# Masks on VectorE, a softmax in three visits and values spread over one stage, in a hybrid decoder step

## The chip, the cores and the metric

One core of one Trainium2 chip runs the kernel. The metric is the device time of one launch in microseconds; the median of the runs counts. Five engines work side by side and meet at semaphores: PE (TensorE, matmuls), DVE (VectorE), ACT (ScalarE), POOL (GpSimd) and SP (SyncE, which only issues DMAs here). Each engine works through its own instructions in a fixed order.

## The reference

One layer of a decoder in which stick-breaking attention and a gated short convolution run in parallel, for one prompt of 512 tokens (with 16 learned tokens ahead) and for 8 sequences that each decode 4 tokens over 512 past positions, which lie in pages of 128. All is float32.

```python
h = rmsnorm(x, g_pre)
q, k, v, ga, cb, cc, ch, gc, ma, mc = jnp.split(h @ w_in, split_offsets(), axis=-1)   # w_in: 2048 x 12288
a = attend(q, k, v, b_sb).reshape(bsz, t, D_ATTN) * jax.nn.silu(ga)
u = cc * ch
u_ext = jnp.concatenate([conv_hist.astype(u.dtype), u], axis=1)
c = cb * causal_conv(u_ext, w_conv, b_conv) * jax.nn.silu(gc)
merged = (jax.nn.sigmoid(ma + b_gate[:D_MODEL]) * (a @ w_pa)
          + jax.nn.sigmoid(mc + b_gate[D_MODEL:]) * (c @ w_pc))
y = x + rmsnorm(merged @ w_out, g_post)
...
def stick_breaking(q, k, v, q_pos, k_pos, b_sb):
    z = jnp.einsum('bqhd,bkhd->bhqk', q, k) * HEAD_DIM ** -0.5 + b_sb[None, :, None, None]
    mask = k_pos[None, :] < q_pos[:, None]
    log_keep = jnp.where(mask, jax.nn.log_sigmoid(-z), 0.0)
    after = lax.cumsum(log_keep, axis=3, reverse=True) - log_keep
    attn = jnp.where(mask, jnp.exp(jax.nn.log_sigmoid(z) + after), 0.0)
    return jnp.einsum('bhqk,bkhd->bqhd', attn, v)
```

D_MODEL is 2048, there are 8 heads of 128, w_pa and w_pc are 1024 x 2048 and w_out is 2048 x 2048. The keys and values of the decoded sequences come from a paged cache through page_table.

## The kernel before, in words

The tokens lie along the free axis: 512 prompt rows and 32 decode rows, 544 queries (TQ). Every float32 operand is split into a high part, rounded to the format that TensorE takes at full rate, and a low part. A product of weights and tokens is then three matmuls: high by high, high by low, low by high. Each weight tile of 128 x 1024 is loaded by SP (w_load), rounded by a ScalarE copy into whi (L235), and VectorE subtracts it to get wlo (L236). TensorE needs both. This split goes on through the whole kernel: 377 such tiles.

The stages, in order:

- Start: norm of the rows, transposes, the first q products. The change does not touch it.
- Heads 0 to 3 are projected and attended at once (head_now); of heads 4 to 7 the projections are stored to DRAM (head_later). In the same time the first of the decode's logits are computed.
- Gates and convolution: the columns of w_in for ga, cb, cc, ch, gc, ma and mc, two column tiles at a time (pair), by a scheme of seven half-size products in place of eight (seven, with the matmuls in product, L849). The sigmoids of ma and mc (ScalarE, L994) go to the DRAM tensor gate_scr.
- The w_pc stage: 16 column tiles (j), each of 48 products in two halves of 272 tokens (L251), which VectorE multiplies with the gate tile gt (L1063) that SP loaded, and which GpSimd's queue writes back to gate_scr (L1064). At j = 0, 3, 6 and 9 the attention of heads 4, 5, 6 and 7 is worked in (HERE, head_here).
- The w_pa stage: the same with the attention's result a_hl; GpSimd's queue loads the two gates' tile back (L1081), which waits for the write of L1064 to the same place.
- The w_out stage (seven again, L849), the transposes back to rows (rows), the squares, and in finish the last norm, the addition of x and the output's DMAs.

The decode part is a Python generator, decode_steps, whose pieces are called in between, so that its instructions land between the products of other stages:

- Logits (L638 to L671): for each sequence and page, q by k as elementwise products on VectorE (L658) and sums on ScalarE and VectorE.
- Softmax in the stick-breaking sense (L672 to L722). For the new rows z_new (32 x 256) and the four pages z_all (128 x 1024) softplus_parts runs on ScalarE: Abs (L404), Exp (L405), Ln (L406), Relu (L407), with the sums on VectorE. Then follow triangular matmuls and an Exp. ScalarE holds one set of function tables at a time: an ACT_TABLE_LOAD stands ahead of a function whose set is not loaded. The Sigmoids of the gates lie in another set than Exp and Ln.
- Values (L724 to L762): 32 pages of values in four blocks (two groups of four sequences, two halves of the heads). Each page is loaded by GpSimd's queue into one of eight vpage buffers. For each of the four sequences of a group a page's matmul (L747) writes its own 32 of the 128 rows of one PSUM tile.

How often the generator is called sets where these pieces stand. During the gates dec_group is called 36 times; the first 29 calls drive one or two pieces of the logits each, the 30th everything up to and with the softmax. In the w_pc stage dec_step(2) runs in each of the 16 steps of j.

The attention of one head (attend, L522): the z products for three groups of key blocks B, C and A, then for each group the softplus steps, the causal mask, and the split into hi (L423) and lo; sums over the later blocks; the products with neg_u and neg_one (L593), which subtract the log sums behind each key; then Exp, the mask again, the split, and the o products with v (L603). The mask is a GpSimd instruction (L550) that sets what is not earlier than the query to zero. Ten masks a head are needed: five blocks, each in r and in A. GpSimd's instructions and the DMAs that it issues stand in one queue.

The planner that orders instructions within an engine keeps a given order where the code pins it (keep_in_program_order, pin).

## Time and profile before

| | |
|---|---|
| median of 3 runs | 1661.16 us (1659.37 to 1664.0) |
| the profiled execution | 1663.13 us, its span 1661.5 us |
| mean granted clock of TensorE | 0.981 |
| busy share of the span | PE 96%, DVE 75%, ACT 59%, POOL 16% |
| moved by DMA | 252.72 MB, mean 152 GB/s |

The span is what the trace covers; the execution's own time is 1.6 us longer. The profile's page gives the busy time of each engine, the span in 40 slices of 41.5 us, the chain of work that ended last, and the costliest groups of instructions. In rows of the trace stand the time in us, the busy time, the engine, the line, the operation, output<-input and the number of instructions; in square brackets the idle time before and what ended it.

### The profile page before, as it was taken

To read this page: it belongs to the slowest core of one execution; us is meant where nothing else is said; L and a number is where in the kernel's file an instruction comes from. 1 tells how busy PE (TensorE), PEld (TensorE's weight loads), DVE (VectorE), ACT (ScalarE), POOL (GpSimd) and SP (SyncE) were. 2 spreads that over 40 slices of the span, in tenths; PEclk is the share of its full clock that TensorE was granted. 3 is DMA by queue.
4 is the path that set the end of the run, shared out by engine and by line. 5 is a ranking of instruction groups with operands and counts; after the bars stand their busy time and mean duration, and the time that the engine had idled before them with its cause. 6 is when DMAs were issued, how large, how long until landed. Compare 5 with 4: busy or idle time off the path is not lost. (4 is left out here: it accounts for less than half of the span.)

```text
span 1661.5 us, 31640 instructions
## 1 busy us (share of the span) xinstructions
PE 1600.6 (96%) x12174; PEld 1540.7 (93%) x12174; DVE 1252.6 (75%) x1669; ACT 974.8 (59%) x2532; POOL 262.7 (16%) x460
## 2 busy tenths in 40 slices
PE   7999999999999999999999999899999979999995
PEld 6999999999999999999999999888878969999995
DVE  4538888797979898988878888865466647877775
ACT  6247887746765656565667677953445533445552
POOL 0033233222101010000011011031232210000002
PEclk7999999999999999999999999999999989999998
DMA  9255545435544444444455454355895535433335
GB/s 225 77 177 155 155 144 160 143 119 171 174 131 128 128 134 129 129 133 134 135 157 170 148 166 143 103 185 163 283 317 169 170 99 174 154 111 94 94 105 193
DMA packets 307468, 252.72 MB, mean 152 GB/s; under 512 B 11569, under 2 KB 276853, under 8 KB 306213
## 3 DMA queue, kind: packets, MB, share of 16 engines
q1 hardware_dynamic: 279269, 161.90, 34.0%
q0 software_dynamic: 28016, 88.80, 16.3%
q8 instruction: 95, 1.56, 0.4%
q14 instruction: 56, 0.46, 0.1%
q10 hardware_dynamic: 32, 0.01, 0.0%
HBM read 217.95 MB, written 32.71 MB: 151 GB/s over the span
## 5 line engine op out<-in xcount | busy, mean ns | idle before, releaser
L235 ACT CAST whi<-raw 128x1024 fp32r<-128x1024 f32 x251 | 262.8, 1049 | 259.7 <-PE o L849 74.3
L236 DVE TENSOR_TENSOR wlo<-raw,whi 128x1024 fp32r<-128x1024 f32 x251 | 306.1, 1220 | 75.6 <-ACT whi L235 57.4
L849 PE MATMUL mm<-h_hi,whi 128*128 128x272 f32 (+1 forms) x1152 | 333.9, 290 | 6.2 <-ACT whi L235 6.2
L849 PE MATMUL mm<-h_lo,whi 128*128 128x272 f32 (+1 forms) x1152 | 332.4, 289 | 0.0
L849 PE MATMUL mm<-h_hi,wlo 128*128 128x272 f32 (+1 forms) x1152 | 332.0, 290 | 0.0
L849 PE MATMUL o<-t_hi,whi 128*128 128x272 f32 (+1 forms) x864 | 253.7, 294 | 7.4 <-DVE c L875 3.0
L849 PE MATMUL o<-t_hi,wlo 128*128 128x272 f32 (+1 forms) x864 | 251.2, 291 | 1.3 <-DVE wlo L236 1.3
L849 PE MATMUL o<-t_lo,whi 128*128 128x272 f32 (+1 forms) x864 | 251.2, 291 | 0.0
L236 DVE TENSOR_TENSOR wlo<-s,whi 128x1024 fp32r<-128x1024 f32 x126 | 154.0, 1222 | 101.3 <-ACT whi L235 101.0
L849 PEld LDWEIGHTS mm<-h_hi,whi 128*128 128x128 f32 x1152 | 217.4, 189 | 10.8 <-ACT whi L235 7.8
L849 PEld LDWEIGHTS mm<-h_lo,whi 128*128 128x128 f32 x1152 | 216.8, 188 | 2.5 <-issue 2.5
L849 PEld LDWEIGHTS mm<-h_hi,wlo 128*128 128x128 f32 x1152 | 216.4, 189 | 2.8 <-issue 2.5
L664 ACT ACTIVATE junk<-pr 128x128 f32<-128x128 f32 x592 | 182.7, 309 | 29.2 <-DVE pr L658 13.4
L235 ACT CAST whi<-s 128x1024 fp32r<-128x1024 f32 x126 | 131.6, 1045 | 100.1 <-PE o L849 32.2
L251 PE MATMUL mm<-h_hi,whi 128*128 128x280 f32 (+1 forms) x640 | 187.1, 293 | 0.0
L251 PE MATMUL mm<-h_hi,wlo 128*128 128x280 f32 (+1 forms) x640 | 187.1, 293 | 0.0
L251 PE MATMUL mm<-h_lo,whi 128*128 128x280 f32 (+1 forms) x640 | 186.7, 292 | 0.0
L849 PEld LDWEIGHTS o<-t_hi,whi 128*128 128x128 f32 x864 | 164.2, 190 | 16.5 <-issue 5.0
L849 PEld LDWEIGHTS o<-t_hi,wlo 128*128 128x128 f32 x864 | 164.4, 190 | 2.3 <-DVE wlo L236 2.2
L849 PEld LDWEIGHTS o<-t_lo,whi 128*128 128x128 f32 x864 | 164.9, 191 | 0.0
L658 DVE TENSOR_TENSOR pr<-kpage,qb 128x1024 f32<-128x1024 f32 x128 | 152.2, 1217 | 7.7 <-DMA kpage<-in_cache_k 3.4
L251 PEld LDWEIGHTS mm<-h_hi,whi 128*128 128x128 f32 x640 | 120.5, 188 | 0.7
(384 smaller groups left out, 3436.2 us busy)
## 6 DMA issues: line engine op xcount, KB each, us to landing
raw<-in_w_in SPq DMA_DIRECT2D x192, 512.0 KB, 4.2
kpage<-in_cache_k POOLq DMA_DIRECT2D x64, 256.0 KB, 3.4
qb<-q_scr POOLq DMA_DIRECT2D x32, 512.0 KB, 5.5
vpage<-in_cache_v POOLq DMA_DIRECT2D x64, 256.0 KB, 5.7
raw<-in_w_out SPq DMA_DIRECT2D x32, 512.0 KB, 4.0
gate_scr<-g POOLq DMA_DIRECT2D x32, 272.0 KB, 3.4
gt<-gate_scr POOLq DMA_DIRECT2D x16, 544.0 KB, 4.1
raw<-in_w_pc SPq DMA_DIRECT2D x16, 512.0 KB, 7.2
```

Source lines behind the costliest of these rows:

```text
L235: act.copy(hi, x)
L236: dve.tensor_sub(lo, x, hi.bitcast(F32))
L251: pe.matmul(o, lhsT=w, rhs=r[:, t0:t1], start=(k == 0 and n == 0), stop=(k == nk - 1 and n == 2))
L658: dve.tensor_mul(pr, kt.unsqueeze(1).broadcast_to([P, 2, 512]), qt))
L664: act.activation(junk, pr[:, t, h * P:(h + 1) * P], AF.Copy, accum_out=z_all[:, pg, b, 4 * hf + h, 2 * i + t:2 * i + t + 1])
L849: pe.matmul(o, lhsT=l[:, k, :], rhs=r, start=(start and k == 0 and m == 0), stop=(stop and k == 7 and m == 2), skip_group_check=True)
```

## The change

It has these parts.

- **Masks on VectorE.** For heads 4 to 7 the mask is one scalar_tensor_tensor on VectorE: the minimum with 3e38, times a tile of zeros and ones (after, which is neg_u plus one). Heads 0 to 3 keep the GpSimd masks.
- **Softplus at one go.** For heads 4 to 7 the four ScalarE steps of all three groups come first, pinned in that order (twelve instructions); the sums, masks and splits follow. softplus_parts is cut in two for that (softplus_acts, softplus_sums). The output's PSUM tile is zeroed by ScalarE, not VectorE.
- **Early inputs.** Head 4's k, q and v are loaded from SP's queue inside the gate stage (at j + w = 14), not behind it; their pool opens when the logits are done, on the side of memory where the decode's tiles lie.
- **The logits at an even rate.** dec_group drives them for 31 calls at the same rates as before; the 32nd call runs what is left of them and the first visit of the softmax.
- **Softmax in three visits**, one for each further call of dec_group: the new rows with pages 3 and 2; pages 1 and 0; the Exps on z_new and on the whole of z_all. Each visit begins with a preload of the tables for Exp and Ln, and its ScalarE steps are pinned.
- **Values spread over w_pc.** dec_step(1 + j % 2) runs in each step, not dec_step(2): 24 calls in 16 steps where 32 were offered. The vpage buffers are seven, not eight.
- **The end.** The 32 rows left over (REST) are transposed into a PSUM tile of their own and kept as 4 strips of 32 rows by 512 columns, so that their addition is one instruction of 128 x 512; their scale is spread over the strips by one small matmul. All additions of finish run on VectorE, in cuts of 1024 or 512 columns; ScalarE and GpSimd share none. The output's DMAs alternate between the queues of SP and ScalarE.

```diff
@@ attend
-                if w > 0:
+                if w > 0 and after is not None:
+                    xm = x[:m, c0:c0 + w]
+                    dve.scalar_tensor_tensor(out=xm, in0=xm, scalar=BIG, in1=after[:m, ts - st * P:ts - st * P + w],
+                                             op0=ALU.min, op1=ALU.mult)
+                elif w > 0:
...
         for g in GROUPS:
-            zt = gt[g]
-            e, l, r, t = tl("e", g), tl("l", g), tl("r", g), tl("lo", g)
-            softplus_parts(e, l, r, t, zt, b)
+            elr[g] = tl("e", g), tl("l", g), tl("r", g)
+            if after is not None:
+                softplus_acts(*elr[g], gt[g], b, pin)
+        for g in GROUPS:
+            (e, l, r), t = elr[g], tl("lo", g)
+            if after is None:
+                softplus_acts(e, l, r, gt[g], b)
+            softplus_sums(e, l, r, t)
             mask(r, g)
...
-        dve.memset(ot, 0.0)
+        if after is None:
+            dve.memset(ot, 0.0)
+        else:
+            act.copy(ot, zero_c.broadcast_to([P, PQ]))
@@ decode_steps
-            tc.keep_in_program_order(act.preload_act_table_set(LNEXP))
...
-            softplus_parts(e[:TS, :BHT], l[:TS, :BHT], rn, t[:TS, :BHT], zn, zero_c[:TS])
-            softplus_parts(e, l, r, t, zf, zero_c)
...
+            for p0 in (2, 0):
+                pin(act.preload_act_table_set(LNEXP))
+                if p0:
+                    softplus_parts(e[:TS, :BHT], l[:TS, :BHT], rn, t[:TS, :BHT], zn, zero_c[:TS], pin)
+                    mask_new(rn)
+                c = slice(p0 * BHT, (p0 + 2) * BHT)
+                softplus_parts(e[:, c], l[:, c], r[:, c], t[:, c], zf[:, c], zero_c, pin)
...
+                yield
+            pin(act.preload_act_table_set(LNEXP))
+            pin(act.activation(zn, zn, AF.Exp))
             mask_new(zn)
-            yield
...
+            pin(act.activation(zf, zf, AF.Exp))
...
-                            vt = d3.tile([P, 512], F32, name="vpage", bufs=8)
+                            vt = d3.tile([P, 512], F32, name="vpage", bufs=7)
@@ dec_group
-        if n <= 29:
+        if n <= 31:
             dec_step(1 if 4 < n <= 20 else 1 + n % 2, "logits")
-        elif n == 30:
-            dec_step(64, "weights")
+        elif n == 32:
+            dec_step(64, "logits")
+            dec_step(1)
@@ gates, w_pc
+            if j + w == 14:
+
+                after = hl[0].tile([P, P], F32, name="after")
+                dve.tensor_scalar_add(after, neg_u.bitcast(F32), 1.0)
+                loaded = head_loads(NOW)
...
-        dec_step(2)
+        dec_step(1 + j % 2)
@@ rows, finish
-                square(4, j, pt[:REST, n:n + P], REST)
-                dve.tensor_mul(og_rest(cs), pt[:REST, n:n + P], g[:REST])
+                square(4, j, pr, REST)
+                r0, c0 = j // 4 * REST, j % 4 * P
+                dve.tensor_mul(ogr[r0:r0 + REST, c0:c0 + P], pr, g[:REST])
...
+                for c0, c1 in zip(cuts[b], cuts[b][1:]):
+                    xc = xs_[i][:, c0:c1]
+                    dve.scalar_tensor_tensor(out=xc, in0=og4[:, i, c0:c1], scalar=rs[:, b:b + 1], in1=xc,
+                                             op0=ALU.mult, op1=ALU.add)
+                    p0, p1, dst = outs[i][0]
+                    next(queues).dma_start(dst[:, c0:c1], xc[p0:p1])
...
-                    if c < 4 - npool[b]:
-                        dve.scalar_tensor_tensor(out=xc, in0=og, scalar=r, in1=xc, op0=ALU.mult, op1=ALU.add)
-                    else:
-                        act.activation(og, og, AF.Copy, scale=r)
-                        pool.tensor_add(xc, xc, og)
...
+                r4 = t_ps()[:, 0:1]
+                pe.matmul(r4, lhsT=to4.rearrange("p a b -> p (a b)"), rhs=rs[:REST, w - 1:w], start=True, stop=True)
+                r4s = op.tile([P, 1], F32, name="r4s")
+                act.copy(r4s, r4)
+                dve.scalar_tensor_tensor(out=xs_[4], in0=ogr, scalar=r4s, in1=xs_[4], op0=ALU.mult, op1=ALU.add)
```

How instructions move is told by their order on each engine, in which lines of the changed kernel have its own numbers (L784 is L747 of before, L614 is L593, L252 is L251, L1094 is L1063, L236 and L237 are L235 and L236, L1032 is L994).

First, GpSimd before, at the end of the w_pc stage, where head 7's masks (L550) stand; L1064 and L1081 are the gate tiles' write and load.

```order
L1064 DMA gate_scr<-gt 128x544
L1081 DMA gt<-gate_scr 128x1088 x2
L550 AFFINE_SELECT r<-r 128x128
L550 AFFINE_SELECT r<-r 16x16
L1064 DMA gate_scr<-gt 128x544
L1081 DMA gt<-gate_scr 128x1088
L550 AFFINE_SELECT r<-r 128x128 x2
```

In the changed order GpSimd has no mask there. Second, VectorE after, at the same place: r and rA are the softplus sums of head 7's groups, L559 is the mask, L432 the split into lo.

```order
L412 TENSOR_TENSOR rA<-rA,lA 128x512
L413 TENSOR_TENSOR r<-r,lo 128x416
L1094 TENSOR_TENSOR gt<-mm,gt 128x272
L237 TENSOR_TENSOR wlo<-raw,whi 128x1024
L413 TENSOR_TENSOR rA<-rA,loA 128x512
L559 SCALAR_TENSOR_TENSOR r<-r,after 128x128 x2
L1094 TENSOR_TENSOR gt<-mm,gt 128x272
L559 SCALAR_TENSOR_TENSOR rA<-rA,after 128x112
L432 TENSOR_TENSOR lo<-r,hi 128x416
L432 TENSOR_TENSOR loA<-rA,hiA 128x512
```

Between the last sum of r (L413) and the first masks of r lie three instructions: a gate product (L1094), a weight split (L237) and the last sum of rA. VectorE takes no part in the masks of this head before.

Third, ScalarE at the softmax. Before, from the full-width Abs on (de, dl and dr are the softmax's tiles, whi the weights' casts, g the gates' Sigmoids):

```order
L404 ACTIVATE de<-z_all,zero_c 128x1024
L405 ACT_TABLE_LOAD
L405 ACTIVATE de<-de 128x1024
L235 CAST whi<-raw 128x1024
L994 ACT_TABLE_LOAD
L994 ACTIVATE g<-mm,bg 128x272
L406 ACT_TABLE_LOAD
L406 ACTIVATE dl<-de,one_c 128x1024
L235 CAST whi<-raw 128x1024
L994 ACT_TABLE_LOAD
L994 ACTIVATE g<-c,bg 128x272
```

After, the first visit from its preload (L735) on to the first Ln:

```order
L735 ACT_TABLE_LOAD
L1032 ACT_TABLE_LOAD
L1032 ACTIVATE g<-o,bg 128x272
L1032 ACTIVATE g<-c,bg 128x272
L404 ACTIVATE de<-z_new,zero_c 32x256
L236 CAST whi<-s 128x1024
L236 CAST whi<-raw 128x1024
L405 ACT_TABLE_LOAD
L405 ACTIVATE de<-de 32x256
L901 ACTIVATE o<-mm 128x272
L406 ACT_TABLE_LOAD
L406 ACTIVATE dl<-de,one_c 32x256
```

Before, the full-width Exp and Ln each stand behind a table load of their own, with a Sigmoid and its load between them. After, the steps on z_all are of half the width and follow in this visit; the preload is followed by a Sigmoid's load and two Sigmoids.

Fourth, TensorE in the w_pc stage. Before, a page of values (L747) with the new rows' products, at the end of a block:

```order
L251 MATMUL mm<-c_hl,whi 128x272 x2
L251 MATMUL mm<-c_hl,wlo 128x272
L747 MATMUL tp<-vpage,z_all 32x512 x4
L747 MATMUL tp<-v_new,z_new 32x512 x4
L251 MATMUL mm<-c_hl,whi 128x272 x2
L251 MATMUL mm<-c_hl,wlo 128x272
```

After, pages (L784) at about the same place in the program, among head 4's products with neg_u (L614):

```order
L784 MATMUL tp<-vpage,z_all 32x512
L252 MATMUL mm<-c_hl,wlo 128x272
L252 MATMUL mm<-c_hl,whi 128x272 x2
L252 MATMUL mm<-c_hl,wlo 128x272
L252 MATMUL mm<-c_hl,whi 128x272 x2
L614 MATMUL z<-hi,neg_u 128x272
L784 MATMUL tp<-vpage,z_all 32x512
L252 MATMUL mm<-c_hl,wlo 128x272
L614 MATMUL z<-hiA,neg_u 128x512
L252 MATMUL mm<-c_hl,whi 128x272 x2
```

Before, four matmuls of pages stand in a row; after, single ones stand between the w_pc products.

More of the change, by code (lines that the diff above doesn't have):

```diff
@@ L671, in decode_steps @@
             yield said
+        hl.append(hlctx.enter_context(tc.tile_pool(name="headin", bufs=1, side="right")))
         BHT = DB * H * DT
@@ L1120, in hybrid_step_kernel @@
     with tc.tile_pool(name="outp", bufs=1) as op:
-        ogr = op.tile([REST, D - CW], F32, name="ogr")
-        def og_rest(cs):
-            return og_a[:REST, 4 * D + cs.start:4 * D + cs.stop] if cs.stop <= CW else \
-                ogr[:, cs.start - CW:cs.stop - CW]
+        ogr = op.tile([P, CW], F32, name="ogr")
+        to4 = op.tile([REST, 4, REST], F32, name="to4")
+        dve.tensor_copy(to4, ident[:REST, :REST].unsqueeze(1).broadcast_to([REST, 4, REST]))
         ssq = og_a[:, 4 * D + CW:4 * D + CW + 5 * KD].rearrange("p (i j) -> p i j", j=KD)
@@ L1238, in hybrid_step_kernel @@
         outs[3] = ((0, np_, yp[t0:PQ, :]), (np_, P, ys))
-        for i in range(5):
+        for i in range(4):
             load_rows(xs_[i], parts[i])
-        finish((0, 1), (1, 1))
+        for c in range(4):
+            nc.sync.dma_start(xs_[4][c * REST:(c + 1) * REST], parts[4][0][2][:, c * CW:(c + 1) * CW])
+        finish((0, 1), ((0, D // 2, D),) * 2)
         both = []
```

93 lines of the change are left out of this document (50 added, 43 removed).

## The prediction

> **What bounds the kernel now.** I read the page first (engine shares, the slices of the granted clock), then TensorE's waits, then the clock in windows round those waits, and then the stretches with the longest waits, engine by engine. From the page, with the shares of the span, and the clock in 40 slices:
>
> ```profile
> PE 1600.6 (96%) x12174; PEld 1540.7 (93%) x12174; DVE 1252.6 (75%) x1669; ACT 974.8 (59%) x2532; POOL 262.7 (16%) x460
> ...
> PEclk7999999999999999999999999999999989999998
> ```
>
> TensorE is busy for 96% of the span, so 61 us of 1661.5 are all that waits can give back, besides what runs at a lower clock. A change that removes no matmul can only win there. The waits of TensorE over the whole span (total us, times, longest):
>
> ```profile
> PE mm L849 <- ACT whi L235: 6.8, 8, 2.6
> ...
> PE z L593 <- ACT hi L423: 4.6, 1, 4.6
> PE mm L251 <- DVE gt L1063: 3.1, 3, 1.4
> ...
> PE o L603 <- ACT hi L423: 1.7, 1, 1.7
> ...
> PE mm L251 <- ACT a_hl L423: 1.4, 1, 1.4
> ```
>
> Three places show here: the gate products (L849) that wait for a weight's cast, the last head's attention (L593, L603, then the first w_pa product that reads its a_hl), and w_pc products that wait for VectorE to empty a PSUM tile (L1063). The start of the kernel holds the rest, and the change does not touch it. A wait costs more than its own length, as two windows show (us, then busy of PE, PEld, DVE, ACT, POOL, the clock, DMA share, GB/s):
>
> ```profile
> 1356.00:1373.00 17.00, 12.90 (x41) 9.70 (x42) 6.94 (x15) 6.17 (x12) 1.81 (x6) 0.50 0.12 35
> ...
> 1062.00:1066.00 4.00, 4.00 (x21) 3.99 (x21) 3.68 (x6) 3.99 (x6) 0.00 (x0) 0.57 0.00 1
> ```
>
> The granted clock was 0.50 for 17 us behind the last head's wait, and about half for 3.4 us (0.57 over 4 us) in the stretch behind a wait of the softmax. A matmul in such a stretch takes twice its time.
>
> **Part 1, the masks on VectorE and the last head.** The stretch in which head 7 ends, GpSimd first, then VectorE, ScalarE and TensorE:
>
> ```profile
> 1346.42 0.57 POOL L1064 DMA_DIRECT2D gate_scr<-gt  x1
> 1354.64 0.54 POOL L1081 DMA_DIRECT2D gt<-gate_scr  x1 [7.65 <-issue]
> 1355.18 0.56 POOL L550 TENSOR_SCALAR_AFFINE_SELECT r<-r 128x128 f32<-128x128 f32 x2
> ```
>
> ```profile
> 1348.60 0.59 DVE L411 TENSOR_TENSOR r<-r,lo 128x416 f32<-128x416 f32 x1
> ```
>
> ```profile
> 1355.77 0.54 ACT L423 CAST hi<-r 128x416 fp32r<-128x416 f32 x1 [8.74 <-POOL r L550]
> ```
>
> ```profile
> 1351.46 0.29 PE L251 MATMUL mm<-a_hl,wlo 128*128 128x272 f32 x1
> ```
>
> The tile r is ready on VectorE at 1349.19. Its mask starts at 1355.18, six microseconds later, though nothing of the mask is late: on GpSimd's queue it stands behind a load of gt (L1081) that waits for the gate_scr write of 1346.42 to land. TensorE starts its last other product at 1351.46. The chain of waits then reads:
>
> ```profile
> 1358.15 3.55 PE z L593 x12
> ...
> 1363.39 5.30 PE o L603 x15
> ...
> 1370.12 90.31 PE mm L251 x705
> ```
>
> From 1351.46 to 1370.12 are 18.7 us. The work in them, with the two z products of 1356.36, is about 10 us at clock 0.50, so 5 us at full clock: 13.7 us are lost. Three more microseconds of w_pa products, to 1373, run at half clock, which loses 1.5. With the change the masks stand on VectorE directly behind r (second order excerpt above), and early inputs put head 7's matmuls further forward: its second mask group now stands among w_pc products, and behind its last z product stand 12 w_pc and 22 w_pa products before the first o product. At 0.128 us each (90.31/705) that covers 4.4 us, more than the 1.7 and 1.4 us that were waited there. What a mask costs VectorE, from the nearest row of the groups of lines (a tensor_tensor of about its width; the new instruction itself is not in this trace):
>
> ```profile
> L570 DVE TENSOR_TENSOR r<-r 128x144 f32<-128x144 f32 x1 | 0.3, 309 | 0.0
> ```
>
> Ten masks a head, two of them of 16 columns, are under 3 us a head, in a stage in which TensorE is the bound: nothing on the path, and up to 2 us if the hi cast of head 7 just misses its place. That chance exists, since "one go" puts all twelve ScalarE steps of the three groups, about 0.55 us each, and two weight casts between z and the first hi cast: roughly 10 us, against about 11 us of products between z and hi in the new order. **Term 1: -13.5 us**, between -9 (a new wait of 3 us and half clock behind it) and -15.
>
> **Part 2, softmax in three visits.** ScalarE in the one visit of before, and TensorE's waits from 1050 to 1110:
>
> ```profile
> 1056.00 1.28 ACT L699 ACT_TABLE_LOAD   x1
> 1057.29 1.28 ACT L994 ACT_TABLE_LOAD   x1
> ...
> 1073.51 1.28 ACT L994 ACT_TABLE_LOAD   x1
> ...
> 1075.31 1.28 ACT L406 ACT_TABLE_LOAD   x1
> 1076.60 1.15 ACT L406 ACTIVATE dl<-de,one_c 128x1024 f32<-128x1024 f32 x1
> ```
>
> ```profile
> PE mm L849 <- ACT whi L235: 3.0, 2, 2.6
> PE o L849 <- ACT whi L235: 2.3, 1, 2.3
> ```
>
> Two waits, of 2.3 and 2.6 us, each behind two table loads in front of a weight cast; with half clock behind each for 3.4 us (1.7 lost each) they cost 8.3 us. The order shows the first pair of loads again in the new first visit: a Sigmoid stands between the preload and the first Exp, in spite of the pins. So the first wait stays. The second pair (1073.51, 1075.31, with the full-width Ln between them and the cast) becomes one load: 2.4 us less ahead of that cast, so that wait shrinks to almost nothing and its half clock goes: -4.3. In all there are 12 loads where 14 stood. Visits two and three add two loads and four half-width steps (about 5 us) or one full Exp to a pair of 21 us in which ScalarE has about 10 to do; I charge +1 for each of them, as 0.3 to 0.9 us waits stand in the profile wherever ScalarE had other work ahead of a cast. **Term 2: -2.3 us**, between -7 and +4.
>
> The Trainium skill (ScalarE: Activation LUTs, What ACT_TABLE_LOAD costs) adds about 1380 ns of drain to each load of 1283 ns; here a second load starts 1.29 us after the first, so this trace shows the load alone. By that page the two loads saved would be worth 5.3 us of ScalarE, not 2.6, and the forecast would fall by some 2 us. The Trainium skill (TensorE: Matmul & The Clock Gate, What's actually happening) has the clock fall after about 3.4 us of idleness; here 2.3 us were enough. By that rule the first wait would cost no clock and the time would be 1.7 us lower.
>
> **Part 3, values spread over w_pc.** No page or product is added, but their places change. TensorE round a single page, and round seven pages in a row (each page is two records):
>
> ```profile
> 1106.00 0.28 PE L849 MATMUL o<-t_hi,wlo 128*128 128x272 f32 x1
> 1106.22 1.04 PE L747 MATMUL tp<-vpage,z_all 128*32 128x512 f32 x2
> 1107.19 0.39 PE L849 MATMUL o<-t_hi,whi 128*128 128x272 f32 x1
> ```
>
> ```profile
> 1262.05 1.92 PE L747 MATMUL tp<-vpage,z_all 128*32 128x512 f32 x14
> 1263.90 0.52 PE L251 MATMUL mm<-c_hl,whi 128*128 128x272 f32 x2
> ```
>
> One page takes 0.97 us from start to the next product, seven take 1.85: pages of different batch elements write different 32 rows of the PSUM tile and run side by side. So the price is per visit, not per page. With the edges (1106.00 to 1107.19 less one product, and a longer product behind) a visit of up to four pages costs 1.17 us. Counted in the order, 31 visits become 36, and single pages 15 become 22, since in the second, third and fourth block of pages many now stand alone. **Term 3: +5.7 us**, between +3 and +8.
>
> The waits for gt (3.1 us) stood beside bursts of pages at 1208 and 1238; an even rate and a GpSimd queue without masks should remove most of them and the half clock at 1240: **term 4: -2.5 us**, between -5 and +5, since VectorE now carries masks there and TensorE meets pages one at a time. The seven buffers instead of eight take away one page of lead; the landing time stands below.
>
> **Part 4, the end.** VectorE's last additions in the view by line (ns, least, median, most), the groups of lines for a 1024-wide operation, and the last microseconds of ScalarE, VectorE and SyncE:
>
> ```profile
> L1169 DVE SCALAR_TENSOR_TENSOR xa<-og_a,rs,xa x7: 733/1743/1756, 1647.6 to 1655.6; 128x512 f32<-128x512 f32 x6, 32x512 f32<-32x512 f32 x1
> ```
>
> ```profile
> L236 DVE TENSOR_TENSOR wlo<-raw,whi 128x1024 fp32r<-128x1024 f32 x50 | 61.1, 1221 | 16.7 <-ACT whi L235 15.6 <-PE z L1144 0.5
> ```
>
> ```profile
> 1645.56 0.27 ACT L1134 ACTIVATE sq<-z 32x128 f32<-32x128 f32 x1 [0.49 <-DVE og_a L1147]
> ```
>
> ```profile
> 1647.55 8.75 DVE L1169 SCALAR_TENSOR_TENSOR xa<-og_a,rs,xa 128x512 f32<-128x512 f32 x7
> 1656.23 0.73 DVE L1169 SCALAR_TENSOR_TENSOR xa<-ogr,rs,xa 32x512 f32<-32x512 f32 x1
> ```
>
> ```profile
> 1656.98 2.32 SPq L1174 DMA_DIRECT2D out<-xa  x5
> ```
>
> The same 512 columns take 733 ns alone and 1743 beside GpSimd's additions. Without GpSimd: three of 1024 columns at 1.22 (estimate, the tensor_tensor's row) and three of 512 at 0.73 are 5.9 us, where 9.4 stood (1647.55 to 1656.96): -3.5. The last square no longer waits for the product on og_a: -0.45. Behind the last addition two issues per queue, some 0.9 us, stand where five took 2.3: -1.4. **Term 5: -5.4 us**, between -4 and -6.5; it is on the path whole, as nothing else runs there. ScalarE's own DMA issues hide behind VectorE's additions; in the first finish they stand in front of casts that wait for TensorE anyway.
>
> Early inputs, the memset moved to ScalarE (0.5 us a head) and the logits' even rate are costed at nothing: all lie under TensorE. **Sum:** -13.5 -2.3 +5.7 -2.5 -5.4 = -18.0. The profiled execution took 1663.13 us, so 1645.1; it lay 2.0 above the median of 1661.16, hence 1643.
>
> **The rivals.**
>
> - *The last head waits again* (0.15). Twelve pinned ScalarE steps delay the first hi cast by 3 us for head 7 and a little for the others; half clock follows. For it: 10 us against 11. Against: heads 5 and 6 have 15 us and more. Term 1 falls to -9, term 4 to 0: 1650.
> - *More comes back* (0.12). The sigmoid between the preloads does no harm, no gt wait is left, single pages fall where TensorE would have waited. Term 2 is -7, term 4 -5: 1636.
> - *Three visits cost more than one* (0.08). Each of three pairs waits 2.3 us behind its loads and loses 1.7 of clock: 12 where 8.3 stood, term 2 is +4, and 1649. The Trainium skill (ScalarE: Activation LUTs, Table sets: the hidden batching unit) asks for all calls of one set before a switch, which speaks for this rival; the one visit of before was not batched either, with its 14 loads. It is also the way in which the change would not do what it says: the pins would hold only in name.
> - *Slower: single pages wait for their DMA* (0.06). Landing of a page in us:
>
> ```profile
> DMA to landing us min/median/max: 3.0/5.7/8.2
> ```
>
> Seven buffers come free in one visit, GpSimd issues seven loads at 0.54 us each, and many single pages follow, each in TensorE's fixed order with everything behind it. The shortest distance between the freeing and the use of a buffer is about 10 us of products, above 8.2, which speaks against it. If each of the 22 single pages waited 1.2 us, 26 us would be added: 1669. It turns the sign from 0.8 us each.
>
> **How the numbers follow.** The forecast's case (0.59) gives 1643, with 1637 to 1650 as its own range. The range for 8 in 10 takes in the two cases at 1649 and 1650 with some of the terms' bounds, and the better one in part: 1634 to 1655. A measurement of this kernel tells some 0.3% (5 us) from no change, so faster means under 1656: all of the first four cases but their upper ends, 0.90. The same: 0.05, from those ends and the mild form of the last rival. Slower: 0.05.
>
> **What would show it.** Right: no GpSimd work between r and hi in head 7, no stretch of 17 us at clock 0.50 behind it, last matmul about 1630, its distance to the end near 12 us instead of 17, additions of 128x512 at 0.73. Part 2: one wait over 2 us near the first visit and none at the second Ln. Part 3: 36 visits of pages, none of them preceded by a DMA wait. Wrong: TensorE waits on hi (head 7), on whi in three pairs, or on vpage; or half clock in w_pc.

## The result, and the profile after

The changed kernel takes 1641.39 us (median of 4 runs, 1639.28 to 1646.64), the kernel before 1662.53 (4 runs, one more than stand in the table of the time before). The ratio is 0.9878, its 95% interval 0.9856 to 0.9899: 21 us less. Ratios here and below leave out slow runs, of which there was one, 5780.48 us of the kernel with eight buffers. The profiled execution took 1641.85 us, 1640.3 of them in the span. From its page, the same two rows as before:

```profile
PE 1594.9 (97%) x12176; PEld 1531.3 (93%) x12176; DVE 1251.8 (76%) x1707; ACT 970.1 (59%) x2529; POOL 232.4 (14%) x414
...
PEclk7999999999999999999999999999999999999998
```

No slice between the start and the end lies below 0.9. Where the time went is seen best stage by stage: windows cut at the first product of the gates, of w_pc, of w_pa, at the last of w_pa and at the last of w_out. Before, then after (us, busy of PE, PEld, DVE, ACT, POOL, the clock, DMA share, GB/s):

```profile
385.10:1194.70 809.60, 794.60 (x6100) 769.49 (x6098) 664.86 (x738) 515.55 (x1336) 96.80 (x168) 1.00 0.51 151
1194.70:1342.80 148.10, 143.94 (x1032) 124.60 (x1032) 92.82 (x181) 75.58 (x129) 42.62 (x76) 0.99 0.68 215
1342.80:1460.30 117.50, 109.15 (x804) 105.63 (x803) 82.24 (x168) 41.05 (x70) 10.75 (x25) 0.93 0.46 142
...
1643.00:1661.50 18.50, 0.73 (x5) 0.27 (x3) 10.96 (x16) 4.54 (x13) 6.74 (x4) 0.59 0.40 128
```

```profile
385.90:1176.20 790.30, 777.70 (x6069) 763.91 (x6067) 662.21 (x737) 510.00 (x1331) 88.72 (x154) 1.00 0.51 152
1176.20:1342.40 166.20, 165.10 (x1084) 128.62 (x1083) 103.00 (x233) 83.69 (x144) 32.94 (x60) 1.00 0.69 215
1342.40:1442.00 99.60, 99.57 (x786) 98.93 (x785) 77.65 (x159) 36.99 (x64) 7.99 (x15) 1.00 0.49 151
...
1624.60:1640.30 15.70, 1.27 (x7) 0.76 (x5) 7.37 (x14) 2.15 (x10) 0.00 (x0) 0.58 0.45 150
```

The gates are 19.3 us shorter and w_pc 18.1 longer: most of that is one thing, pages that moved from the one stage to the other. What is left is w_pa, 17.9 shorter, with its clock back from 0.93 to 1.00, and the end, 2.8 shorter. The waits of TensorE that answer to the rows of before:

```profile
PE o L887 <- ACT o L901: 5.9, 5, 3.1
PE mm L887 <- ACT whi L236: 3.3, 5, 0.7
PE tp L1208 <- DVE rs L137: 2.8, 1, 2.8
...
PE mm L252 <- DVE gt L1094: 1.1, 1, 1.1
```

No wait for hi is left in the last head. The softmax's wait is there once, with 3.1 us and under another name (o, L901). The 2.8 us in L1208 are the small new matmul at the end, on which nothing but the last addition waits. In head 7 the first masks of r start 2.0 us behind its last sum (1327.77 and 0.58, then 1330.36), where 6.0 stood before; the hi cast follows (VectorE, ScalarE):

```profile
1327.77 0.58 DVE L413 TENSOR_TENSOR r<-r,lo 128x416 f32<-128x416 f32 x1
...
1330.36 0.48 DVE L559 SCALAR_TENSOR_TENSOR r<-r,after 128x128 f32<-128x128 f32 x2
```

```profile
1330.88 0.54 ACT L431 CAST hi<-r 128x416 fp32r<-128x416 f32 x1 [2.36 <-DVE r L559]
```

### The profile page after: what moved, and what is told of

It reads as the page before. It is cut to its first block, busy times and chain, and to the rows that moved or that the text cites. A ratio compares the mean times of both kernels' runs of the same rounds, so it can differ in the third digit from the quotient of the medians.

```text
span 1640.3 us, 31584 instructions
## 1 busy us (share of the span) xinstructions
PE 1594.9 (97%) x12176; PEld 1531.3 (93%) x12176; DVE 1251.8 (76%) x1707; ACT 970.1 (59%) x2529; POOL 232.4 (14%) x414
## 4 chain that ended last, share of the span: by engine, by line
PE 75%; ACT 6%; DMA 5%; DVE 5%; issue 3%; POOL 0%; DVEq 0%; SPq 0%; POOLq 0%; ACTq 0%
PE mm L887 24%; PE mm L252 24%; PE o L887 19%; ACT junk L695 3%; PE tp L784 2%; ACT whi L236 2%; DMA raw<-in_w_in 2%; PE z L614 1%; PE o L624 1%; DVE pr L689 1%; DVE wlo L237 1%; DMA gt<-gate_scr 1%; PE z L545 1%; PE z L887 1%; DMA kpage<-in_cache_k 1%
## 5 line engine op out<-in xcount | busy, mean ns | idle before, releaser
L236 ACT CAST whi<-raw 128x1024 fp32r<-128x1024 f32 x251 | 263.1, 1050 | 258.5 <-PE o L887 79.3
L237 DVE TENSOR_TENSOR wlo<-raw,whi 128x1024 fp32r<-128x1024 f32 x251 | 306.4, 1221 | 58.0 <-ACT whi L236 46.1
L237 DVE TENSOR_TENSOR wlo<-s,whi 128x1024 fp32r<-128x1024 f32 x126 | 154.2, 1224 | 101.5 <-ACT whi L236 101.2
L236 ACT CAST whi<-s 128x1024 fp32r<-128x1024 f32 x126 | 131.6, 1044 | 97.5 <-PE o L887 31.0
L252 PE MATMUL mm<-h_hi,whi 128*128 128x280 f32 (+1 forms) x640 | 187.1, 293 | 0.0
L252 PE MATMUL mm<-h_hi,wlo 128*128 128x280 f32 (+1 forms) x640 | 187.0, 293 | 0.0
L252 PE MATMUL mm<-h_lo,whi 128*128 128x280 f32 (+1 forms) x640 | 186.7, 292 | 0.0
L252 PEld LDWEIGHTS mm<-h_hi,whi 128*128 128x128 f32 x640 | 120.5, 188 | 0.7
```

Of the source, the lines that this page charges most:

```text
L236: act.copy(hi, x)
L237: dve.tensor_sub(lo, x, hi.bitcast(F32))
L252: pe.matmul(o, lhsT=w, rhs=r[:, t0:t1], start=(k == 0 and n == 0), stop=(k == nk - 1 and n == 2))
```

## The experiments

Twelve kernels were run. Their times are medians, compared with the kernel before in the same session (1659 to 1662 us). A difference from the changed kernel compares medians of two sessions, between which the kernel before moved by up to 3.4 us (1659.15 to 1662.53), so a few us alone show nothing. First those that take apart head 7.

**Masks on GpSimd again** (x1_masks_gpsimd: all else as changed).

```diff
-                if w > 0 and after is not None:
+                if w > 0 and after is False:
```

> The changed kernel with the masks of heads 4 to 7 on GpSimd again, everything else as changed. Theory (the masks' place behind GpSimd's load of a gate tile was the cause of the last head's wait): head 7's second and third group of neg_u products fall behind the first w_pa products again, TensorE waits 3 to 5 us for a hi cast there and runs at clock 0.50 behind it for 7 to 17 us; 8 to 14 us more, 1649 to 1655. Rival (softplus at one go or the early inputs gained it, the masks' engine does not matter): no such wait, 1641, within 3.

Measured 1648.37, ratio to before 0.9929 (0.9905 to 0.9953): 7 us above the changed kernel, but not for the reason expected. The w_pa stage and two waits:

```profile
1343.90:1448.20 104.30, 102.76 (x802) 101.18 (x801) 78.86 (x161) 39.87 (x68) 9.27 (x20) 1.00 0.48 149
```

```profile
PE mm L252 <- DVE gt L1094: 5.1, 2, 3.9
...
PE mm L252 <- ACT a_hl L431: 1.4, 1, 1.4
```

The stage costs 4.7 us more, 2 of them head 7's own products that are back in it. There is no wait for hi over 0.2 us and no half clock in it. The largest other item is a wait of 3.9 us for gt in the middle of w_pc, with one window of half clock behind it. So the masks' engine alone did not bring the wait of before back.

**Softplus group by group, masks on VectorE** (x2_by_group).

```diff
-            if after is not None:
-                softplus_acts(*elr[g], gt[g], b, pin)
...
-            if after is None:
-                softplus_acts(e, l, r, gt[g], b)
+            softplus_acts(e, l, r, gt[g], b)
```

> The changed kernel with softplus group by group (as before the change), masks still on VectorE. Theory (masks are the cause): no wait of TensorE for hi over 0.5 us in head 7 and no stretch at clock 0.50; 34 visits of value pages where 36 stand, so 1639, within 3. Rival (one go is what brings head 7's products forward): a wait of 2 to 5 us for hi in head 7 with half clock behind it, 1646 to 1655.

Measured 1641.84 (ratio 0.9882, 0.9856 to 0.9907). The w_pa stage is 99.5 us at clock 1.00, as in the changed kernel. One go is not what removed the wait either.

**Both undone** (x8_neither: the two edits above together).

```diff
-                if w > 0 and after is not None:
+                if w > 0 and after is False:
...
-            if after is not None:
-                softplus_acts(*elr[g], gt[g], b, pin)
```

> The changed kernel with both undone: masks of heads 4 to 7 on GpSimd, and softplus group by group. Theory (either of the two alone keeps head 7's products among w_pc products, each hides the other): now all three groups of head 7's neg_u products stand among the w_pa products, TensorE waits 4 us or more for hi or r there, with clock 0.50 behind it, and the w_pa stage is 10 to 18 us longer than in the changed kernel (99.6); 32 visits of pages for 36, -4: 1647 to 1656. Rival (the gain came from elsewhere, the two parts are worth what they are worth singly, about +3 and 0): 1640 to 1645.

Measured 1647.22 (ratio 0.9927, 0.9902 to 0.9951):

```profile
1335.60:1446.70 111.10, 107.97 (x804) 105.68 (x803) 83.53 (x171) 41.70 (x71) 11.53 (x25) 0.94 0.46 143
```

The w_pa stage is 11.5 us longer than in the changed kernel and its clock 0.94. Each of the two parts hides what the other does: undone singly they cost the stage 5 us and nothing, together 11.5. The total rises by only 6: w_pc is 4 us shorter, 2.3 of them head 7's products that moved to w_pa, and all that lies ahead of the gates took 2.3 us less in this profile.

**The masks alone, on the kernel before** (b2_masks_only).

```diff
-                if w > 0:
+                if w > 0 and after is not None:
+                    xm = x[:m, c0:c0 + w]
+                    dve.scalar_tensor_tensor(out=xm, in0=xm, scalar=BIG, in1=after[:m, ts - st * P:ts - st * P + w],
+                                             op0=ALU.min, op1=ALU.mult)
+                elif w > 0:
...
     loaded = head_loads(NOW)
+    after = hl.tile([P, P], F32, name="after")
+    dve.tensor_scalar_add(after, neg_u.bitcast(F32), 1.0)
```

> The kernel before with one edit: the masks of heads 4 to 7 on VectorE. TensorE's order has head 7's last groups at the same place as before the change, behind 45 and 63 w_pa products. Theory of the prediction (r waited for its mask in GpSimd's queue behind the load of a gate tile): the mask no longer waits, the hi cast is 4 us or more earlier, the w_pa stage falls from 117.5 to 104 to 109 and the time to 1648 to 1654. Rival (the place in TensorE's order decides, not the mask's engine: behind 63 products the chain from z to a_hl has nothing left to hide it): TensorE still waits 3 us or more in head 7 with half clock behind it, the w_pa stage stays over 112, 1656 to 1662.

Measured 1652.38 (ratio 0.9956, 0.9943 to 0.9969). Both theories hold a part:

```profile
1341.20:1450.90 109.70, 106.57 (x804) 104.22 (x803) 84.23 (x177) 41.07 (x70) 7.95 (x15) 0.95 0.46 145
```

```profile
PE o L608 <- ACT hi L424: 1.7, 1, 1.7
PE mm L252 <- ACT a_hl L424: 1.4, 1, 1.4
```

The wait of 4.6 us for hi is gone: the mask did hang in GpSimd's queue behind the load of gt, and that is worth 7.8 us of the stage. The waits of 1.7 and 1.4 us behind it stay, with three windows at half clock, and the stage is 10 us above the changed kernel's 99.6, 2.3 of them head 7's own products. They go with the place of head 7's products, as the table below shows.

**The even logits alone, on the kernel before** (b1_even_logits).

```diff
-        if n <= 29:
+        if n <= 31:
...
-        elif n == 30:
+        elif n == 32:
```

> The kernel before with one edit: the logits at the even rate until the 31st call, and the softmax in its one visit at the 32nd. Theory (the softmax's second wait of 2.6 us went because the visit stands at another place of the gate products, not because there are three visits): between the last logit and the first page no wait of TensorE above 1 us but one of about 3 us, gate stage without pages 4 to 8 us shorter; TensorE's order has 39 visits of pages for 31, +8.6, head 7 as planned at the end of w_pc for part of its waits: 1652 to 1662. Rival (the place does not matter, the steps' width and the loads do): the waits of 2.3 and 2.6 us both stand, 1663 to 1670.

Measured 1648.36 (ratio 0.9926, 0.9901 to 0.9952), better than expected. The second wait of the softmax fell to 0.7 us, as expected of the place; the first is 3.1 us. What was not expected is the w_pa stage:

```profile
1345.50:1445.00 99.50, 99.47 (x786) 98.83 (x785) 77.70 (x158) 37.56 (x64) 10.52 (x20) 1.00 0.49 151
```

It has lost all of its 18 us, with the masks on GpSimd and softplus by groups. The edit touches nothing of head 7. It moves the logits, the softmax and the pages, and the planner then put head 7's products further forward; why it did so is not shown. The seven kernels in one table; the second column is how many w_pa products stand ahead of head 7's last group in TensorE's order:

| kernel | w_pa products ahead | w_pa stage, us | clock in it |
|---|---|---|---|
| before | 63 | 117.5 | 0.93 |
| both undone | 63 | 111.1 | 0.94 |
| before, masks alone | 63 | 109.7 | 0.95 |
| masks on GpSimd again | 35 | 104.3 | 1.00 |
| by group / even logits alone / changed | 0 | 99.5 / 99.5 / 99.6 | 1.00 |

The time follows the place: the kernel before and the one with even logits have the same code for head 7 and differ by 18 us in this stage, and a kernel further down (two calls in every step) lies between, with 14 products ahead and 102.6 us. The mask's queue adds up to 8 us where the place is bad (117.5 to 109.7), but only 1.4 in the kernel with both undone (111.1 to 109.7).

**Head 4's inputs late again** (x6_late_inputs).

```diff
-                loaded = head_loads(NOW)
...
+    loaded = head_loads(NOW)
     for k in range(0, 8, 2):
```

> The changed kernel with head 4's k, q and v loaded behind the gates again (their pool and the mask tile stay where they are). TensorE's order is the same in the w_pc stage. Theory of the prediction (the early inputs lie under TensorE and are worth nothing): 1641, within 3. Rival (at the start of w_pc the DMA engines are full, and these loads hold up the small ones that VectorE waits for): a wait of TensorE for gt of 2 to 5 us near 1180 with half clock behind it, 1644 to 1648.

Measured 1640.70 (ratio 0.9892, 0.9874 to 0.9910): no difference, and TensorE's order in w_pc is the same. The early inputs are worth nothing here and move nothing.

**Softmax in one visit** (x3_one_visit: the old code in the changed kernel, at the 32nd call).

```diff
-            dec_step(64, "logits")
-            dec_step(1)
+            dec_step(64, "weights")
```

> The changed kernel with the softmax in one visit, as before the change, at the 32nd call. Theory (three visits spread the table loads and the wide steps): the second wait for a weight cast, of about 2.6 us, comes back, and the waits between the logits' end and the first page sum to 5 us or more where the changed kernel has about 4; with half clock behind them up to 8 us more, less 4 us for 32 visits of pages where 36 stand: 1641 to 1646. Rival (the waits are the same, and the two stretches of half clock that went were a matter of where a wait fell in TensorE's clock windows of 3.41 us): waits as in the changed kernel, only the pages change, 1637.

Measured 1635.04 (ratio 0.9853, 0.9827 to 0.9879): the rival, and 6 us better than the changed kernel (4 by the ratios, whose intervals overlap; the runs, 1634.43 to 1638.73, do not). Its waits, and ScalarE ahead of the cast that waited before:

```profile
PE o L881 <- ACT o L895: 5.3, 5, 3.1
...
PE mm L881 <- ACT whi L236: 3.9, 6, 0.7
```

```profile
1090.48 1.28 ACT L1026 ACT_TABLE_LOAD   x1
1091.78 0.49 ACT L1026 ACTIVATE g<-mm,bg 128x272 f32<-128x272 f32 x1
1092.29 1.28 ACT L406 ACT_TABLE_LOAD   x1
1093.58 1.15 ACT L406 ACTIVATE dl<-de,one_c 128x1024 f32<-128x1024 f32 x1
```

Two loads with a Sigmoid between them and the full-width Ln stand in front of the cast, as before the change, but TensorE waits 0.7 us there, not 2.6. What differs from before is the place among the gate products. Three visits gained nothing on the waits, and they cost pages: they use up two more calls, and in the order that follows stand 36 visits of pages, 22 of them single (49.3 us with their edges), where one visit of the softmax leaves 32, of which 14 are single (43.3 us).

**Two calls in every step of w_pc** (x4_two_calls).

```diff
-        dec_step(1 + j % 2)
+        dec_step(2)
```

> The changed kernel with two calls of the generator in every step of w_pc, as before the change. Theory (a visit of up to four pages costs what one page costs): TensorE's order has 42 visits of pages where 36 stand, so 6 x 1.08 = 6.5 us more: 1648, within 3. Rival (the even rate itself matters, two calls bring bursts that wait for VectorE's gt or for page loads): 1650 to 1656 with waits of TensorE on gt or vpage. Second rival (price per page): 1641.

Measured 1645.86 (ratio 0.9919, 0.9895 to 0.9943). The 42 visits sum to 56.1 us in the trace, 6.8 more than 36; the median rose by 4.5, the profiled span by only 2.7. TensorE did not wait in w_pc at all, but 14 w_pa products now stand ahead of head 7's last group and the w_pa stage takes 3 us more. More calls gave more single pages.

**Pages in fours** (x5_fours).

```diff
-                        for j in range(4):
+                        for j in (3, 2, 1, 0):
                             vt = d3.tile([P, 512], F32, name="vpage", bufs=7)
                             page_load(vt, vc, 4 * g + j, pg, cs)
-                            vts.append(vt)
+                            vts.insert(0, vt)
...
-                        pe.matmul(po[32 * j:32 * (j + 1), :], ...
+                        pin(pe.matmul(po[32 * j:32 * (j + 1), :], ...
```

> The changed kernel with the four pages of a group loaded in reverse order and their matmuls pinned in program order, so that the first matmul waits for the page that lands last and the four stand together: 14 visits of pages in TensorE's order where 36 stand (11 of 4, 2 of 8, one of 20). Theory (a visit of up to four pages costs 1.08 us, as one page does): 11 x 1.08 + 2 x 2.0 + 5 us = 21 us of pages where the changed kernel has 41.6; 20 us less, 1621, within 4. First rival (the price is per page): no change, 1641, within 4. Second rival (each group now waits for its last page's landing): TensorE waits on vpage for 0.5 us or more in many of the 14 visits, and over half of the gain is lost, 1631 or more.

Measured 1644.46 (ratio 0.9894, 0.9867 to 0.9922): the second rival. A visit of four did cost 1.1 to 1.3 us with its edges where nothing was waited for. But the groups became late: the planner put the last 16 pages, with four products of the new rows, in one block among the w_pa products (20.3 us from 1328.6). Three of the four waits for page loads, 10.8 us of 12.6, stand in that block:

```profile
PE tp L784 <- DMA vpage<-in_cache_v: 12.6, 4, 4.4
```

**Fours, one visit, eight buffers, late inputs, two calls** (y_late8_one_fours_two). The eighth buffer stands where head 4's inputs were held early.

```diff
-                            vt = d3.tile([P, 512], F32, name="vpage", bufs=7)
+                            vt = d3.tile([P, 512], F32, name="vpage", bufs=8)
...
-                loaded = head_loads(NOW)
...
-        dec_step(1 + j % 2)
+        dec_step(2)
```

The softmax in one visit and the pages in fours are edited as in the two kernels above.

> The changed kernel with the softmax in one visit, head 4's inputs loaded behind the gates again (so eight vpage buffers fit), the pages of a group loaded in reverse order and pinned, and two calls in every step: 14 visits of pages (8 of four, 6 of eight). Theory (price per visit; with two whole groups of buffers the loads of one group run under the other): 8 x 1.1 + 6 x 2.05 = 21 us of pages where the one-visit kernel has 36 at 1635: 1620, within 4. Rival (the reverse order makes each group wait for a late landing, as in the kernel with seven buffers): waits of TensorE on vpage of 2 us or more and half clock behind them, 1630 to 1645.

Measured 1635.66 (ratio 0.9849, 0.9819 to 0.9879). The pages fell to 24.2 us in 14 visits, and 19 us were gained there against the one-visit kernel; all of it was lost again. VectorE waited for a load of 256 KB, and TensorE then for VectorE (4.2 us) and for a copy by ScalarE that stood behind it (6.3 us), with half clock behind both:

```profile
1183.48 0.69 DVE L1060 TENSOR_TENSOR sg<-sg 128x512 f32<-128x512 f32 x1 [6.42 <-DMA sg<-a_scr]
...
1269.41 0.69 DVE L1060 TENSOR_TENSOR sg<-sg 128x512 f32<-128x512 f32 x1 [7.78 <-DMA sg<-a_scr]
```

```profile
1176.00:1180.00 4.00, 4.00 (x35) 4.00 (x34) 1.06 (x1) 1.60 (x2) 0.55 (x1) 1.00 1.04 380
1180.00:1184.00 4.00, 1.76 (x15) 1.54 (x13) 0.52 (x1) 0.00 (x0) 0.00 (x0) 1.00 1.03 378
```

The DMA share is over 1.0 at 380 GB/s: pages, gate tiles and weights fill the engines (head 4's inputs were issued before, from 1165.8 to 1169.2), and that load, issued at 1174.4, landed at 1183.4.

**The same with seven buffers and the early inputs kept** (y_one_fours_two: the one-visit kernel, the fours, and this line).

```diff
-        dec_step(1 + j % 2)
+        dec_step(2)
```

> The changed kernel with the softmax in one visit, pages of a group loaded in reverse order and pinned, two calls in every step, seven buffers, early inputs kept: 17 visits of pages (14 of four, 3 of eight). Theory (price per visit, and the early inputs keep the small loads of the w_pc stage's start out of a full DMA): 14 x 1.1 + 3 x 2.05 = 22 us of pages where the one-visit kernel has 36, no wait over 2 us near 1180: 1622, within 5. Rival (bursts of four pages fill the DMA engines, and small loads or pages come late wherever they collide): waits of 3 us or more with half clock, 1630 to 1640.

Measured 1626.27 (4 runs, 1624.10 to 1626.93), ratio to before 0.9803 (0.9784 to 0.9823): 15 us below the changed kernel, the quickest of all. Four pages as one row of TensorE (8 records), and the one long wait left in w_pc:

```profile
1235.92 1.06 PE L779 MATMUL tp<-vpage,z_all 128*32 128x512 f32 x8
1242.75 1.06 PE L779 MATMUL tp<-vpage,z_all 128*32 128x512 f32 x8
```

```profile
PE tp L787 <- ACT ob L784: 3.7, 1, 3.7
```

Seventeen visits cost 23.5 us where the changed kernel has 49.3. Of these 26 us 15 reached the time: TensorE is busy for 1575.2 us where it was for 1594.9, and idle for 3.6 us more. The long wait goes back again to VectorE, which waited 5.3 us for sg from a_scr at 1260 and then 3.8 for gt. The two kernels differ in the early inputs and the eighth buffer; with seven and early the wait near 1180 is 1.1 us, not 4.2. Which of the two does it was not taken apart.

**One queue for the output** (x7_one_queue).

```diff
-            queues = cycle((nc.sync, act))
+            queues = cycle((nc.sync,))
```

> The changed kernel with all output DMAs of finish on SP's queue. From the last addition's end to the end of the span are 6.0 us in the changed kernel, 4.6 before. Theory (the quicker additions bring 2.4 MB of output into 9 us, and the DMA engines' rate of about 400 GB/s sets the end, whatever queue issues): the end stays within 0.6 us of 6.0, the last issues still take long, 1641 within 3. Rival (two queues that issue at once slow each other, 1.6 us for the last issues where one queue takes 0.4): 1.4 us or more less behind the last addition. Second rival (the two queues help): 1 us or more longer.

Measured 1641.66 (ratio 0.9909, 0.9880 to 0.9939). Its end, and that of the changed kernel:

```profile
1633.40 0.75 DVE L1211 SCALAR_TENSOR_TENSOR xa<-ogr,r4s,xa 128x512 f32<-128x512 f32 x1
```

```profile
1628.60 5.00 DVE L1200 SCALAR_TENSOR_TENSOR xa<-og_a,rs,xa 128x1024 f32<-128x1024 f32 x5
1633.52 0.74 DVE L1211 SCALAR_TENSOR_TENSOR xa<-ogr,r4s,xa 128x512 f32<-128x512 f32 x1
```

From the last addition's end to the end of the span are 5.8 us with one queue (to 1639.96) and 6.0 with two (to 1640.26). The queue does not matter. The changed kernel's DMA engines while the output leaves:

```profile
1632.00:1634.00 2.00, 0.00 (x0) 0.00 (x0) 2.00 (x4) 0.00 (x0) 0.00 (x0) 0.50 1.06 365
```

They are full at 365 GB/s, and about 0.9 busy at 270 GB/s in the next four us. Before, the slower additions spread the same output over more time, at 155 to 307 GB/s.

## Why the prediction was right, point by point

The forecast was 1643 us, the measurement is 1641.39. The profile's difference is 21.2 us, and the terms were:

| term | forecast | measured in the profile |
|---|---|---|
| 1, head 7 | -13.5 | -15.6 (w_pa -17.9, of which 18 of head 7's products, 2.3, moved to w_pc) |
| 2, softmax | -2.3 | -4.6 (waits 5.4 to 3.8, and two windows of half clock, 1.5 each) |
| 3, pages | +5.7 | +6.6 (visits 42.7 to 49.3 us, a gt wait of 1.4 taken out before) |
| 4, gt | -2.5 | -3.5 (waits 3.1 to 1.1, one window of half clock) |
| 5, the end | -5.4 | -2.8 |

Together -19.9; the 1.3 us left over are not assigned. Terms 1 and 5 lie outside their own bounds (-9 to -15 and -4 to -6.5). That the sum came within 2 us is in part luck: terms 1, 2 and 4 brought 5.4 us more than forecast, the end 2.6 and the pages 0.9 less. Three of the terms came out near for reasons that were in part wrong. In the prediction a matmul at half clock "takes twice its time", and a window costs 1.7 us; the last section shows 1.8 times and 1.5 us.

**Term 1.** That the mask "stands behind a load of gt" was right as a mechanism (the masks alone take 7.8 us from the stage), but the step "early inputs put head 7's matmuls further forward" failed: with late inputs the order is the same and so is the time. So did the step that the even rate is "costed at nothing": alone on the kernel before it takes all 18 us from the w_pa stage and 12 us (by the ratio) from the time. No part brings the place by itself in every setting: in the changed kernel the masks without one go leave no w_pa product ahead of head 7's last group and one go without the masks leaves 35, the masks alone on the kernel before leave 63, and so does the even rate with both undone. In size, the working of this term counts 13.7 and 1.5 us lost, 15.2 in all, and 15.6 came; why -13.5 was written is not said there. The rival "the last head waits again" did not come: the products between z and hi were enough, as the order showed.

**Term 2.** The step that failed is "becomes one load: 2.4 us less ahead of that cast, so that wait shrinks to almost nothing". With the pair left as it was the wait is 0.7 us too. It shrank because the 32nd call lies at another place of the gate products. That the first wait stays, because a Sigmoid stands between the preload and the first Exp, was right; it was 3.1 us. That it cost no half clock in this profile was luck, as the last section shows. The +1 charged for visits two and three was not seen as waits (nothing over 0.5 us there); their true price is pages.

**Term 3.** Price and count were right: 36 visits, with both edges 1.17 us for one page, 1.19 for four and 2.04 for seven (five visits more at 1.17 are 5.9, not the 5.7 written). The cause of the single pages was put too simply: x3 and x4 show that each change of calls deals them out anew (32, 36, 42), and pinned groups of four halve the cost. The rival "single pages wait for their DMA" did not come here (0.6 us, once); it came where they were forced into fours.

**Term 5.** The additions were as worked out (5.7 us for 9.4, forecast 5.9) and so was the earlier last square (0.5). The step that failed is "two issues per queue, some 0.9 us". Each queue's last two:

```profile
1634.30 2.29 ACTq L1214 DMA_DIRECT2D out<-xa  x2
```

```profile
1634.29 2.13 SPq L1214 DMA_DIRECT2D out<-xa  x2
```

They end 2.3 us behind the last addition, as the five of before did, and from there to the end of the span are 3.7 us where 2.2 stood: 6.0 for 4.6 in all. Since the end comes no later with one queue, and the DMA engines are about 0.9 busy meanwhile, it is the transfers that take the time and not their issue. From the last product to the end are 14.5 us, where the prediction named 12 as a sign of being right.

**Term 4** came out near the forecast in this profile, but it is not safe: with small edits (x1, x2) a wait of 3.2 to 3.9 us for gt stood in the middle of w_pc, near 1257.

## What to carry to other kernels

Count visits, not instructions: where several small matmuls run side by side in TensorE, what costs is each time that it is entered (here 1.17 us for one page and 1.19 for four), so keep the group together, and check that its loads do not fill the DMA engines just when another load is waited for. Where a planner sets the order, read from the order how many independent products stand behind a chain's last step; an edit that seems to act through one queue may act only by moving that place, and two such edits do not add up. A quicker engine ahead of a burst of output gains only what the DMA engines can take.

## What the runs showed of the hardware

**The clock gate works on a fixed grid.** In every profile the stretches of half clock start and end on one grid of 3.413 us that runs through the whole execution; only its phase differs from run to run. The same wait at the softmax (3.1 us) stands in 12 of the profiles. It was followed by no half clock in three of them, by one window in five and by two in four. The changed kernel's wait lies across a border of the grid, the one of x1 nearly inside a window; both with one window of the grid and the next:

```profile
1077.60:1081.00 3.40, 1.66 (x14) 1.44 (x12) 1.55 (x2) 3.38 (x6) 1.08 (x2) 1.00 1.13 345
1081.00:1084.40 3.40, 1.99 (x15) 1.99 (x16) 2.22 (x3) 3.36 (x6) 0.00 (x0) 1.00 0.12 49
```

```profile
1075.96:1079.37 3.41, 1.02 (x9) 0.80 (x7) 2.23 (x2) 3.38 (x5) 0.78 (x2) 1.00 1.01 328
1079.37:1082.78 3.41, 2.67 (x12) 2.67 (x13) 2.01 (x5) 3.38 (x6) 0.00 (x0) 0.50 0.09 28
```

TensorE idles 1.7 and 1.4 us in the two windows of the first, and 2.4 in the one of the second. Counted over the 14 profiles are the windows of the grid between 40 and 1600 us that ran at full clock themselves. All 23 with 1.87 us or more without a matmul were followed by half clock, 7 of 15 between 1.7 and 1.87, and 3 of 58 between 0.9 and 1.7. In x1's trace products start 0.126 us apart ahead of the wait (1076.06 to 1076.69) and 0.227 apart at half clock behind it (1080.50 to 1081.86):

```profile
1076.06 0.29 PE L887 MATMUL mm<-h_hi,whi 128*128 128x272 f32 x1
...
1076.69 0.29 PE L887 MATMUL mm<-h_hi,wlo 128*128 128x272 f32 x1
1080.11 0.60 PE L887 MATMUL o<-t_hi,whi 128*128 128x272 f32 x1 [3.13 <-ACT o L901]
1080.50 0.43 PE L887 MATMUL o<-t_lo,whi 128*128 128x272 f32 x1
...
1081.86 0.43 PE L887 MATMUL o<-t_lo,whi 128*128 128x272 f32 x1
```

That is 1.8 times, so a window of half clock that is full of products costs 1.5 us. A wait of 3.1 us may thus cost nothing more, and one of 2 us within one window 1.5 more. It may also spread the runs: the changed kernel's run of 1646.64 us had a mean clock of 0.986, the three others 0.990. That is not shown, since two runs of x1 with mean clocks of 0.995 and 0.988 took the same 1648.35 us.

The Trainium skill (TensorE: Matmul & The Clock Gate, What's actually happening) has the window of 3413 ns and that it runs free of the kernel; the traces agree. It has the clock fall after at least one idle window; the traces differ, 1.87 us within one window were enough in every case.

**Loads behind a full DMA** land late: 9 us for 256 KB in the kernel with eight buffers, 5.7 us in the median for a page in the kernel before.
